# Two heads of an output tile: sums over keys in turns on the halves of the array, retention scores on half rows

## The chip, the cores and the metric

The program runs on one core of a Trainium2 chip. The metric is the device time of one execution in microseconds; several runs of the same program are given by their median.

## The reference, cut to what matters

Two transformer-like blocks run one after the other on 512 tokens of width 1024, in float32. Three attention-like parts are touched by the change:

- **Retention** (first block, 8 heads of 64): the scores q·k are multiplied by a fixed decay of the distance (zero above the diagonal) and then summed over the keys against v, without a softmax; the kernel does this over all 512 tokens at once.
- **NSA** (first block, 8 query heads in 2 key groups): three attentions per head are added with gates: over compressed blocks, over selected blocks and over a window. With 512 tokens the last two are causal softmax attentions with keys and values of their own.
- **MLA** (second block, 8 heads, 96 wide for scores, 64 for values): one causal softmax attention.

```
scores = q @ k.T * decay;  o = scores @ v                  # retention
o = g0 * softmax(q @ kc.T) @ vc + g1 * softmax(q @ ks.T) @ vs + g2 * softmax(q @ kw.T) @ vw   # NSA
o = softmax(q @ k.T / sqrt(96)) @ v                        # MLA
```

## The kernel before, in words

Activations lie transposed: channels on the 128 partitions, 512 tokens along the row. An output tile of an attention is 128 channels x 512 tokens and holds two heads: one on partitions 0 to 63, one on 64 to 127. I call them the low and the high head.

**Softmax attention** (`attn_head`, L406 to L432). For one head and each of four query tiles i of 128 queries: the scores `att_s` over 128(i+1) keys and a mask (L221, the helper behind every `self.mm`), the maximum `att_nm` on VectorE (L419), the exponential `att_e` with its sum on ScalarE (L422), the reciprocal (L424), the scaling (L426 or L428), transposes on TensorE into `att_pt` (L431), and a copy on ScalarE into `PT` (L432), which so holds the probabilities with keys on partitions. `att_pt` has one PSUM bank (`tpc=1`), `att_s` two (`smc=2`), `att_e` three buffers, `PT` two. After the four tiles of a head come its four **sums over keys**, products of 64 value columns with 512, 384, 256 and 128 query columns, into the half of the output tile that is the head's. In NSA (tiles `nsa_o`, p = 0 to 3) the low head comes first with its compressed part (`pct`, `vcz`), then its selected part "s", then its window part "w", and then the high head with the same three; in MLA (`mla_o`) one head after the other. Each output tile is one PSUM bank (`oc=1`).

**Retention** (p = 0 to 3, two heads each). Four projections (`raw`, `project`: three products for each of eight chunks, L216 to L218), rotary embedding, and for each key tile j and each head: scores `ret_s`, a product with the decay `dec` on VectorE into `ret_P` (L686), and the sum `ret_o`. Keys `rk` of both heads lie on 128 rows; the queries are kept twice in `qz`, with zeros on the rows of the other head, so that every score uses all 128 rows of the array. `ret_s` shares two banks with other small products. Behind each p the rows of a modulation vector are summed up (`ada_rows`: 16 loads, ScalarE, GpSimd).

Float32 products are issued as two matmul instructions each; so a head's sums are eight.

**What sets the order.** The order on each engine isn't written by hand. A scheduler walks a simulated time line and, on each engine, takes the instruction of the lowest number among those whose inputs it holds to be there. Numbers follow the program, but an `ahead` block moves them: NSA of p = 0 counts from 4000 before the first retention group, NSA of p = 1 to 3 from the start of retention group p, and MLA, like the preparation of the recurrent part beside it, from a point far ahead in the second block, so that projections of gates fill what they leave. Instructions on one PSUM tile keep the program's order. Transfers are issued on SP's queue in one such order, weights, `dec` and modulation rows alike.

Of the kernel before, what the change touches and what calls it, by code (L numbers as in the profile page):

```python
# [11 lines left out]
F32 = mybir.dt.float32  # L12
# [6 lines left out]
OP = mybir.AluOpType  # L19
# [3 lines left out]
T = 512  # L23
# [135 lines left out]
PRE = ("kc", "vc")  # L159
MS = 2  # L160
PL = ()


class Kernel:
# [238 lines left out]
            nc.tensor.transpose(ps[:, b, :rows], src[:rows, b * 128:(b + 1) * 128], self.cst("ident")[:rows, :rows])  # L403
        nc.scalar.activation(dst, ps[:, :, :rows], AF.Copy)

    def attn_head(self, qk, gate, PT, wk):  # L406

        nc = self.nc  # L410
        for i in range(4):
            n = 128 * (i + 1)
            ps = self.ps([128, T], "att_s")
            w = max(n, 256) if len(qk) > 1 else n
            for j, (q, k) in enumerate(qk):
                self.mm(ps[:, :w], q[:, i * 128:(i + 1) * 128], k[:, :w], j == 0, False)
            self.mm(ps[:, n - 128:n], self.identb, self.maskb, False, True)
            nm = wk.tile([128, 1], F32, name="att_nm", bufs=4)
            nc.vector.tensor_reduce(nm, ps[:, :n], AX.X, OP.max, negate=True)  # L419
            e = wk.tile([128, T], F32, name="att_e", bufs=3)  # L420
            z = wk.tile([128, 1], F32, name="att_z", bufs=4)
            nc.scalar.activation(e[:, :n], ps[:, :n], AF.Exp, bias=nm, accum_out=z)  # L422
            rz = wk.tile([128, 1], F32, name="att_rz", bufs=4)
            nc.vector.reciprocal(rz, z)  # L424
            if gate is None:
                nc.vector.tensor_scalar(e[:, :n], e[:, :n], rz, None, op0=OP.mult)  # L426
            else:
                nc.vector.tensor_scalar(e[:, :n], e[:, :n], rz, gate(i), op0=OP.mult, op1=OP.mult)  # L428
            pt = self.ps([128, 4, 128], "att_pt", "tp")
            for j in range(i + 1):  # L430
                nc.tensor.transpose(pt[:, j, :], e[:, j * 128:(j + 1) * 128], self.cst("ident"))  # L431
            nc.scalar.activation(PT[:, 0:i + 1, i, :], pt[:, 0:i + 1, :], AF.Copy)  # L432

# [25 lines left out]
    def first(self):  # L459
        nc, a = self.nc, self.a  # L460
# [3 lines left out]
        lo_, hi_, full = slice(0, 64), slice(64, 128), slice(0, 128)  # L464
# [10 lines left out]
        tab = {nm: tuple(p.tile([128, T], F32, name=k + nm) for k in ("cos_", "sin_")) for nm, p in (("r", hp), ("n", tp))}  # L475
# [10 lines left out]
        with self.tc.high_priority(offset=5000):  # L486
# [4 lines left out]
            r = self.norm_r(xs, twk, True, True)  # L491
# [10 lines left out]
        wk = self.pool(hid, "wk1")  # L502
# [6 lines left out]
        def raw(name, scale=1.0):  # L509
            o = project(name)  # L510
            q = wk.tile([128, T], F32, name="q_raw", bufs=3)
            nc.scalar.activation(q, o, AF.Copy, scale=scale)
            return q
# [9 lines left out]
        qs = nk.tile([128, 8, T], F32R, name="qs")  # L523
        kk = {nm: nk.tile([128, 2, T], F32R, name="kk" + nm) for nm in "sw"}
        kl = {nm: nk.tile([128, T], F32R, name="kl" + nm) for nm in "sw"}
        vt = {nm: nk.tile([128, 4, 128], F32, name="vt" + nm) for nm in "sw"}
        gt = nk.tile([128, 4, 32], F32, name="gt")
# [10 lines left out]
        for kv, nm in enumerate(("kc", "vc")):  # L538
# [3 lines left out]
            for g in range(2):  # L542
                gr = slice(g * 64, g * 64 + 64)
# [7 lines left out]
            for m in range(16):  # L551
# [3 lines left out]
                for g in range(2):  # L555
                    r = 2 * kv + g
# [7 lines left out]
        w = self.ring("w_raw")  # L564
        nc.sync.dma_start(w, a["w_in"][idx["ngl"]])
        o = self.ps([128, T], "pj", "pj")
        for c in range(NC8):
            r = slice(c % 4 * 32, c % 4 * 32 + 32)
# [87 lines left out]
        rp = self.pool(ns, "ret")  # L656
# [5 lines left out]
        n0 = []  # L662
        for p in range(4):
            n0.append(self.tc.cur_priority)
            qz = rp.tile([128, 2, T], F32, name="qz", bufs=2)
            nc.gpsimd.memset(qz[hi_, 0, :], 0.0)
            nc.gpsimd.memset(qz[lo_, 1, :], 0.0)
            self.rope_T(raw(f"rq{p}"), self.cst("perm_r"), *tab["r"], [(qz[lo_, 0, :], lo_), (qz[hi_, 1, :], hi_)], wk)
            rk = rp.tile([128, T], F32, name="rk", bufs=2)
            self.rope_T(raw(f"rk{p}"), self.cst("perm_r"), *tab["r"], [(rk, full)], wk)  # L670
            rv = rp.tile([128, 4, 128], F32, name="rv", bufs=2)
            self.to_tokens(raw(f"rv{p}"), 128, rv)
            og = project(f"rg{p}")
            th = wk.tile([128, T], F32, name="th", bufs=2)
            nc.scalar.activation(th, og, AF.Tanh, scale=0.5)
            nc.vector.scalar_tensor_tensor(mix[:, p, :], th, 1.0, og, op0=OP.add, op1=OP.mult)
            dec = rp.tile([128, 2, T], F32, name="dec", bufs=2)
            nc.sync.dma_start(dec, a["dec"][:, 2 * p:2 * p + 2, :])
            po = self.ps([128, T], "ret_o", "o")
            for j in range(4):  # L680
                n = T - 128 * j
                for par in range(2):
                    sc = self.ps([128, T], "ret_s")
                    self.mm(sc[:, :n], rk[:, j * 128:(j + 1) * 128], qz[:, par, j * 128:])
                    P = rp.tile([128, T], F32, name="ret_P", bufs=3)
                    nc.vector.tensor_tensor(P[:, :n], sc[:, :n], dec[:, par, :n], op=OP.mult)  # L686
                    self.mm(po[par * 64:par * 64 + 64, j * 128:], rv[:, j, par * 64:par * 64 + 64], P[:, :n], j == 0, j == 3)
            oc = rp.tile([128, T], F32, name="ln_o")
            nc.scalar.activation(oc, po, AF.Copy)
            mu = self.ps([128, T], "ln_mu")  # L690
            self.mm(mu, self.cst("bd64"), oc)
            nc.vector.tensor_tensor(oc, oc, mu, op=OP.subtract)
            sq = rp.tile([128, T], F32, name="ln_sq")
            nc.scalar.activation(sq, oc, AF.Square)
            self.ln_exp()
            var = self.ps([128, T], "ln_var")
            self.mm(var, self.cst("bd64"), sq)
            rs = rp.tile([128, T], F32, name="ln_rs")
            nc.scalar.activation(rs, var, AF.Ln, bias=self.col(5))
            nc.scalar.activation(rs, rs, AF.Exp, scale=-0.5)  # L700
            t = rp.tile([128, T], F32, name="ln_t")
            nc.vector.tensor_scalar(sq, var, 1e-5, None, op0=OP.add)
            self.newton(rs, sq, t)
            nc.vector.scalar_tensor_tensor(t, oc, 0.5, rs, op0=OP.mult, op1=OP.mult)
            nc.vector.tensor_tensor(mix[:, p, :], t, mix[:, p, :], op=OP.mult)

            if p == 0:
                self.ada_rows(a["w_ada"], self.silu1, self.v("b_ada"), mod, 2048, rp, self.ps([128, NC8], "ada_ps", TAG))
                nc.vector.tensor_tensor(self.gg, mod[:, 16:24], self.v("g_post"), op=OP.mult)
            elif p < 3:  # L710
                self.ada_rows(a["w_ada2"], self.silu2, self.v("b_ada2"), self.mod2, (p - 1) * 1024, rp, self.ps([128, NC8], "ada_ps", TAG))
# [3 lines left out]
        for p in range(4):  # L715
            with self.ahead(self.tc.cur_priority - n0[QP[p][0]] - QP[p][1]):
                po = self.ps([128, T], "nsa_o", "o")
                for g in range(2):
                    h = p + 4 * g
                    gr = slice(g * 64, g * 64 + 64)  # L720
                    self.mm(po[gr, :], vcz[:, g, p, :], pct[:, g, :], True, False)
                    for ai, nm in ((1, "s"), (2, "w")):
                        PT = np_.tile([128, 4, 4, 128], F32, name="PT", bufs=2)
                        self.attn_head([(qs[:, h, :], kk[nm][:, g, :]), (qs[gr, h, :], kl[nm][gr, :])], lambda i: gt[:, i, h * 3 + ai:h * 3 + ai + 1], PT, np_)
                        for j in range(4):
                            self.mm(po[gr, j * 128:], vt[nm][:, j, gr], PT[:, j, j:, :], False, ai == 2 and j == 3)
                nc.vector.scalar_tensor_tensor(mix[:, 4 + p, :], po, 0.5, mix[:, 4 + p, :], op0=OP.mult, op1=OP.mult)
        ns.close()
# [83 lines left out]
    def second(self):  # L812
# [279 lines left out]
        with self.ahead(self.tc.cur_priority - n0):  # L1092
            at = self.pool(ax, "mla_at")
            for p in range(4):
                po = self.ps([128, T], "mla_o", "o")
                for par in range(2):
                    h = 2 * p + par
                    PT = at.tile([128, 4, 4, 128], F32, name="PT", bufs=2)
                    self.attn_head([(qf[0:96, h, :], kf[0:96, h, :])], None, PT, at)
                    for j in range(4):  # L1100
                        self.mm(po[par * 64:par * 64 + 64, j * 128:], vt[:, j, h * 64:(h + 1) * 64], PT[:, j, j:, :],
                                j == 0, j == 3)
                nc.scalar.activation(qf[:, 2 * p, :], po, AF.Copy)
# [917 lines left out]
```

## Time and profile before

| | |
|---|---|
| runs | 1384.52, 1402.33, 1398.66 us; median 1398.66 |
| profiled execution | 1399.72 us, its span 1397.9 us (1.8 us lie around it) |
| TensorE (PE) busy | 1285.6 us, 92% of the span |
| VectorE (DVE), ScalarE (ACT), GpSimd (POOL) busy | 859.1 us (61%), 617.6 us (44%), 274.0 us (20%) |
| mean granted TensorE clock | 0.963 of full speed |
| chain of work that ended last | PE 72%, DMA 8%, DVE 7%, ACT 6% |

A busy time counts a matmul from its start to its modelled end, and matmuls overlap in the pipeline: what one costs in a dense stream is the distance from its start to the next start. Retention and NSA lie between 157 and 440 us of the span, MLA between 678 and 803 us.

### The profile page before, as it was taken

To read this page: it belongs to the slowest core of one execution; us is meant where nothing else is said; L and a number is where in the kernel's file an instruction comes from. 1 tells how busy PE (TensorE), PEld (TensorE's weight loads), DVE (VectorE), ACT (ScalarE), POOL (GpSimd) and SP (SyncE) were. 2 spreads that over 40 slices of the span, in tenths; PEclk is the share of its full clock that TensorE was granted. 3 is DMA by queue.
4 is the path that set the end of the run, shared out by engine and by line. 5 is a ranking of instruction groups with operands and counts; after the bars stand their busy time and mean duration, and the time that the engine had idled before them with its cause. 6 is when DMAs were issued, how large, how long until landed. Compare 5 with 4: busy or idle time off the path is not lost.

```text
span 1397.9 us, 20781 instructions
## 1 busy us (share of the span) xinstructions
PE 1285.6 (92%) x7765; PEld 1009.1 (72%) x7765; DVE 859.1 (61%) x1971; ACT 617.6 (44%) x1204; POOL 274.0 (20%) x237
## 2 busy tenths in 40 slices
PE   4899999999998999999999899988998779998887
PEld 1468656566556986887677578887997777888777
DVE  6646553754764555444867764647574965997832
ACT  5234453655453557334465644545333543342010
POOL 0000140423000100000000034434000214436560
PEclk9999999999999999999999979999999999999799
DMA  9532341333111113223332154545233536878564
GB/s 346 192 99 76 122 150 60 121 121 106 61 68 61 46 63 107 83 83 106 113 106 91 61 155 148 174 129 159 84 100 106 173 106 194 329 256 307 168 216 120
DMA packets 92110, 187.56 MB, mean 134 GB/s; under 512 B 11084, under 2 KB 37260, under 8 KB 92000
## 3 DMA queue, kind: packets, MB, share of 16 engines
q1 hardware_dynamic: 77744, 143.84, 32.2%
q0 software_dynamic: 14256, 42.30, 8.9%
q8 instruction: 63, 1.03, 0.3%
q14 instruction: 47, 0.39, 0.1%
HBM read 178.94 MB, written 16.78 MB: 140 GB/s over the span
## 4 chain that ended last, share of the span: by engine, by line
PE 72%; DMA 8%; DVE 7%; ACT 6%; issue 3%; POOL 2%; SPq 0%; ACTq 0%; DVEq 0%; POOLq 0%
PE pj L216 11%; PE pj L217 11%; PE pj L218 11%; PE y L221 6%; DMA ada_w<-in_w_ada 5%; PE att_s L221 4%; PE nsa_o L221 3%; PE lv L221 3%; PE att_pt L431 2%; POOL ada_acc L300 2%; PE ret_s L221 2%; PE ret_o L221 2%; PE mr L221 1%; PE mla_o L221 1%; ACT ada_w L298 1%
## 5 line engine op out<-in xcount | busy, mean ns | idle before, releaser
L216 PE MATMUL pj<-hh,w_hi 128*128 128x512 f32 (+1 forms) x736 | 284.1, 388 | 15.6 <-ACT hh L357 8.2
L217 PE MATMUL pj<-hl,w_hi 128*128 128x512 f32 (+1 forms) x736 | 282.5, 384 | 2.9 <-DVE hl L358 2.9
L218 PE MATMUL pj<-hh,w_lo 128*128 128x512 f32 (+1 forms) x736 | 282.2, 384 | 0.4 <-DVE w_lo L211 0.4
L300 POOL TENSOR_TENSOR ada_acc<-ada_acc,ada_w 128x512 f32<-128x512 f32 x98 | 130.5, 1337 | 380.1 <-ACT ada_w L298 361.6
L211 DVE TENSOR_TENSOR w_lo<-w_raw,w_hi 128x1024 fp32r<-128x1024 f32 (+1 forms) x108 | 133.0, 1234 | 102.2 <-ACT w_hi L210 93.4
L216 PEld LDWEIGHTS pj<-hh,w_hi 128*128 128x128 f32 x736 | 141.1, 192 | 48.9 <-issue 11.3
L210 ACT ACTIVATE w_hi<-w_raw 128x1024 fp32r<-128x1024 f32 (+1 forms) x112 | 114.4, 1025 | 128.7 <-PE pj L217 103.3
L217 PEld LDWEIGHTS pj<-hl,w_hi 128*128 128x128 f32 x736 | 141.1, 192 | 32.9 <-DVE hl L358 6.6
L218 PEld LDWEIGHTS pj<-hh,w_lo 128*128 128x128 f32 x736 | 140.8, 191 | 28.6 <-issue 3.0
L298 ACT ACTIVATE ada_w<-ada_w,silu 128x512 f32<-128x512 f32 x98 | 70.4, 722 | 97.1 <-DMA ada_w<-in_w_ada 94.5
L221 PE MATMUL y<-dg,up 128*128 128x128 f32 x768 | 101.1, 295 | 12.6 <-DMA up<-in_eu,gix 5.6
L221 PEld LDWEIGHTS y<-dg,up 128*128 128x128 f32 x768 | 97.7, 210 | 14.7 <-DMA up<-in_eu,gix 5.8
L419 DVE TENSOR_REDUCE att_nm<-att_s 128x1 f32<-128x128 f32 (+1 forms) x96 | 46.6, 486 | 73.3 <-PE att_s L221 72.9
L432 ACT ACTIVATE PT<-att_pt 128x128 f32<-128x128 f32 (+1 forms) x96 | 41.7, 434 | 89.8 <-PE att_pt L431 89.7
L1411 DVE SCALAR_TENSOR_TENSOR junk<-dn,htok 128x1024 f32<-128x1024 f32 x48 | 58.5, 1219 | 15.4 <-DMA dn<-in_ed_rows,gix 10.7
L422 ACT ACTIVATE att_e<-att_s,att_nm 128x128 f32<-128x128 f32 (+1 forms) x96 | 50.5, 526 | 11.2 <-DVE att_nm L419 10.5
L431 PE MATMUL att_pt<-consts,att_e 128*128 128x128 f32 x240 | 44.6, 285 | 4.4 <-ACT PT L432 2.7
L1405 POOL DMA_INDIRECT dn<-in_ed_rows,gix x32 | 34.9, 1092 | 59.3 <-DVE gix L1444 36.6
L431 PEld LDWEIGHTS att_pt<-consts,att_e 128*128 128x128 f32 x240 | 29.1, 141 | 23.0 <-issue 8.5
L216 PE MATMUL pj<-oh,w_hi 128*128 128x256 f32 x128 | 39.8, 311 | 2.9 <-DVE m_g L1157 2.9
L1405 POOL DMA_INDIRECT up<-in_eu,gix x32 | 35.5, 1109 | 14.3 <-issue 8.2
L217 PE MATMUL pj<-ol,w_hi 128*128 128x256 f32 x128 | 37.7, 295 | 0.0
(617 smaller groups left out, 2701.6 us busy)
## 6 DMA issues: line engine op xcount, KB each, us to landing
ada_w<-in_w_ada SPq DMA_DIRECT2D x144, 256.0 KB, 3.3
w_raw<-in_w_in SPq DMA_DIRECT2D x65, 512.0 KB, 3.8
w_raw<-in_w_out SPq DMA_DIRECT2D x24, 512.0 KB, 4.0
w_raw<-in_w_query SPq DMA_DIRECT2D x16, 512.0 KB, 5.5
w1t<-in_cmp_w SPq DMA_DIRECT2D x8, 512.0 KB, 4.2
gate_d<-g_t SPq DMA_DIRECT2D x16, 256.0 KB, 2.0
w_raw<-in_w_o_rwkv SPq DMA_DIRECT2D x8, 512.0 KB
x<-in_xT SPq DMA_DIRECT2D x4, 512.0 KB, 8.6
```

Of the source, the lines that this page charges most:

```text
L210: self.nc.scalar.activation(hi, src, AF.Copy)
L211: (eng or self.nc.vector).tensor_tensor(lo, src, hi, op=OP.subtract)
L216: self.nc.tensor.matmul(ps, wh, xh, start=(i == 0), stop=False)
L217: self.nc.tensor.matmul(ps, wh, xl, start=False, stop=False)
L218: self.nc.tensor.matmul(ps, wl, xh, start=False, stop=(i == n - 1))
L221: self.nc.tensor.matmul(ps, l, r, start=start, stop=stop)
L298: nc.scalar.activation(wt if k else t, wt, AF.Copy, scale=s[:, k:k + 1])
L300: nc.gpsimd.tensor_tensor(t, t, wt, op=OP.add)
L422: nc.scalar.activation(e[:, :n], ps[:, :n], AF.Exp, bias=nm, accum_out=z)
L431: nc.tensor.transpose(pt[:, j, :], e[:, j * 128:(j + 1) * 128], self.cst("ident"))
L1405: nc.gpsimd.indirect_dma_start(out=g, out_offset=None, in_=a[table], in_offset=bass.IndirectOffsetOnAxis(ap=ix, axis=0), **more)
L1411: nc.vector.scalar_tensor_tensor(junk, g, 1.0, h, op0=OP.mult, op1=OP.mult, accum_out=out)
```

## The change

For each output tile, both heads are now taken through the softmax before any of their sums over keys, and the sums then alternate: low head j = 0, high head j = 0, low head j = 1, and so on. In NSA this is done for the selected part of both heads and then for the window part, and the compressed parts of both heads come first. `PT` has three buffers. In MLA `att_e` has two buffers in place of three, and the small columns three in place of four. In retention the queries `rq` are kept once, the scores of a head are a product over its own 64 rows, the scores of both heads are issued before both products with the decay, and the sums alternate. The zero fills of `qz` are gone, one of two additions of the rotary embedding of q as well, and `dec` has one buffer in place of two.

```diff
+NPT = 3
...
-    def attn_head(self, qk, gate, PT, wk):
+    def attn_head(self, qk, gate, PT, wk, eb=3, sb=4):
...
-            e = wk.tile([128, T], F32, name="att_e", bufs=3)
-            z = wk.tile([128, 1], F32, name="att_z", bufs=4)
+            e = wk.tile([128, T], F32, name="att_e", bufs=eb)
+            z = wk.tile([128, 1], F32, name="att_z", bufs=sb)
...
-            qz = rp.tile([128, 2, T], F32, name="qz", bufs=2)
-            nc.gpsimd.memset(qz[hi_, 0, :], 0.0)
-            nc.gpsimd.memset(qz[lo_, 1, :], 0.0)
-            self.rope_T(raw(f"rq{p}"), self.cst("perm_r"), *tab["r"], [(qz[lo_, 0, :], lo_), (qz[hi_, 1, :], hi_)], wk)
+            rq = rp.tile([128, T], F32, name="rq", bufs=2)
+            self.rope_T(raw(f"rq{p}"), self.cst("perm_r"), *tab["r"], [(rq, full)], wk)
...
-            dec = rp.tile([128, 2, T], F32, name="dec", bufs=2)
+            dec = rp.tile([128, 2, T], F32, name="dec")
...
+                scs, Ps = [], []
+                for gr in (lo_, hi_):
+                    sc = self.ps([128, T], "ret_s")
+                    self.mm(sc[:, :n], rk[gr, j * 128:(j + 1) * 128], rq[gr, j * 128:])
+                    scs.append(sc)
                 for par in range(2):
-                    sc = self.ps([128, T], "ret_s")
-                    self.mm(sc[:, :n], rk[:, j * 128:(j + 1) * 128], qz[:, par, j * 128:])
                     P = rp.tile([128, T], F32, name="ret_P", bufs=3)
-                    nc.vector.tensor_tensor(P[:, :n], sc[:, :n], dec[:, par, :n], op=OP.mult)
-                    self.mm(po[par * 64:par * 64 + 64, j * 128:], rv[:, j, par * 64:par * 64 + 64], P[:, :n], j == 0, j == 3)
+                    nc.vector.tensor_tensor(P[:, :n], scs[par][:, :n], dec[:, par, :n], op=OP.mult)
+                    Ps.append(P)
+                for gr, P in zip((lo_, hi_), Ps):
+                    self.mm(po[gr, j * 128:], rv[:, j, gr], P[:, :n], j == 0, j == 3)
...
-                for g in range(2):
-                    h = p + 4 * g
-                    gr = slice(g * 64, g * 64 + 64)
+                for g, gr in enumerate((lo_, hi_)):
                     self.mm(po[gr, :], vcz[:, g, p, :], pct[:, g, :], True, False)
-                    for ai, nm in ((1, "s"), (2, "w")):
-                        PT = np_.tile([128, 4, 4, 128], F32, name="PT", bufs=2)
-                        self.attn_head([(qs[:, h, :], kk[nm][:, g, :]), (qs[gr, h, :], kl[nm][gr, :])], lambda i: gt[:, i, h * 3 + ai:h * 3 + ai + 1], PT, np_)
-                        for j in range(4):
+                for ai, nm in ((1, "s"), (2, "w")):
+                    PTs = []
+                    for g, gr in enumerate((lo_, hi_)):
+                        h = p + 4 * g
+                        PTs.append(np_.tile([128, 4, 4, 128], F32, name="PT", bufs=NPT))
+                        self.attn_head([(qs[:, h, :], kk[nm][:, g, :]), (qs[gr, h, :], kl[nm][gr, :])], lambda i: gt[:, i, h * 3 + ai:h * 3 + ai + 1], PTs[g], np_)
+                    for j in range(4):
+                        for gr, PT in zip((lo_, hi_), PTs):
                             self.mm(po[gr, j * 128:], vt[nm][:, j, gr], PT[:, j, j:, :], False, ai == 2 and j == 3)
...
-                for par in range(2):
-                    h = 2 * p + par
-                    PT = at.tile([128, 4, 4, 128], F32, name="PT", bufs=2)
-                    self.attn_head([(qf[0:96, h, :], kf[0:96, h, :])], None, PT, at)
-                    for j in range(4):
+                PTs = []
+                for h in (2 * p, 2 * p + 1):
+                    PTs.append(at.tile([128, 4, 4, 128], F32, name="PT", bufs=NPT))
+                    self.attn_head([(qf[0:96, h, :], kf[0:96, h, :])], None, PTs[-1], at, 2, 3)
+                for j in range(4):
+                    for par, PT in enumerate(PTs):
+                        h = 2 * p + par
                         self.mm(po[par * 64:par * 64 + 64, j * 128:], vt[:, j, h * 64:(h + 1) * 64], PT[:, j, j:, :],
                                 j == 0, j == 3)
```

## Rows read from the trace of the kernel before

**Rows 1.** Busy time by stretch: stretch and length, then each engine, clock, DMA.
```profile
157.00:440.00 283.00, 274.74 (x1138) 166.11 (x1139) 160.15 (x333) 145.57 (x313) 59.54 (x46) 0.98 0.29 93
678.00:803.00 125.00, 119.47 (x531) 81.73 (x530) 88.18 (x241) 75.33 (x185) 0.00 (x0) 1.00 0.28 93
```

**Rows 2.** Groups by line on PE: busy us, mean ns, idle before.
```profile
L221 PE MATMUL ret_s<-qz,rk 128*128 128x512 f32 (+3 forms) x64 | 24.3, 472 | 0.0
L221 PE MATMUL ret_o<-ret_P,rv 128*64 128x512 f32 (+3 forms) x64 | 23.7, 458 | 0.0
...
L221 PE MATMUL nsa_o<-PT,vts 128*64 128x512 f32 (+3 forms) x64 | 20.6, 468 | 1.1 <-ACT PT L432 1.1
...
L221 PE MATMUL mla_o<-PT,vt 128*64 128x512 f32 (+3 forms) x64 | 18.9, 439 | 1.2 <-ACT PT L432 1.2
```

**Rows 3.** Timeline of PE, 736 to 740 us: start, length, what.
```profile
736.36 0.40 PE L217 MATMUL pj<-hl,w_hi 128*128 128x512 f32 x1
736.59 0.40 PE L218 MATMUL pj<-hh,w_lo 128*128 128x512 f32 x1
736.91 2.37 PE L221 MATMUL mla_o<-PT,vt 128*64 128x512 f32 x8
739.21 0.33 PE L431 MATMUL att_pt<-consts,att_e 128*128 128x128 f32 x1
```

**Rows 4.** Timeline of PE, 418 to 421 us.
```profile
418.39 1.93 PE L221 MATMUL nsa_o<-PT,vtw 128*64 128x512 f32 x5
419.95 0.64 PE L221 MATMUL nsa_o<-pct,vcz 128*64 128x512 f32 x1
420.16 0.49 PE L221 MATMUL nsa_o<-PT,vtw 128*64 128x256 f32 x2
...
420.96 0.33 PE L431 MATMUL att_pt<-consts,att_e 128*128 128x128 f32 x1
```

**Rows 5.** Timeline of PE, 880 to 882 us: products over 64 rows, later stage.
```profile
880.02 0.60 PE L221 MATMUL mr<-AR,KA 64*128 64x256 f32 x4
880.45 0.59 PE L221 MATMUL mr<-AR,BE 64*128 64x256 f32 x2
880.88 0.59 PE L221 MATMUL mr<-AR,KA 64*128 64x256 f32 x2
881.41 0.33 PE L1206 MATMUL r_tp<-consts,AR 128*128 128x128 f32 x1
```

**Rows 6.** Timeline of PE, 258 to 280 us, retention and NSA of p = 1.
```profile
258.45 1.88 PE L221 MATMUL ret_s<-qz,rk 128*128 128x512 f32 x4
...
260.86 1.07 PE L221 MATMUL nsa_o<-pct,vcz 128*64 128x512 f32 x2
...
262.23 1.07 PE L221 MATMUL ret_o<-ret_P,rv 128*64 128x512 f32 x2
...
268.22 1.07 PE L221 MATMUL ret_o<-ret_P,rv 128*64 128x512 f32 x2
...
277.20 2.37 PE L221 MATMUL nsa_o<-PT,vts 128*64 128x512 f32 x8
```

**Rows 7.** Timeline of DVE, 260 to 264 us.
```profile
260.78 0.68 DVE L686 TENSOR_TENSOR ret_P<-ret_s,dec 128x512 f32<-128x512 f32 x1
...
263.11 0.68 DVE L686 TENSOR_TENSOR ret_P<-ret_s,dec 128x512 f32<-128x512 f32 x1
```

**Rows 8.** Timeline of ACT: the fourth copies into PT of two successive heads.
```profile
271.79 0.60 ACT L432 ACTIVATE PT<-att_pt 128x512 f32<-128x512 f32 x1 [2.66 <-PE att_pt L431]
...
296.44 0.57 ACT L432 ACTIVATE PT<-att_pt 128x512 f32<-128x512 f32 x1
```

**Rows 9.** Timeline of ACT, 766 to 772 us, two exponentials of one MLA head.
```profile
766.67 0.57 ACT L422 ACTIVATE att_e<-att_s,att_nm 128x384 f32<-128x384 f32 x1
...
771.46 0.69 ACT L422 ACTIVATE att_e<-att_s,att_nm 128x512 f32<-128x512 f32 x1
```

**Rows 10.** Timeline of SP's queue, 226 to 227 us.
```profile
226.19 0.38 SPq L678 DMA_DIRECT2D dec<-in_dec  x1
```

More of the change, by code (lines that the diff above doesn't have):

```diff
@@ L417, in attn_head @@
             self.mm(ps[:, n - 128:n], self.identb, self.maskb, False, True)
-            nm = wk.tile([128, 1], F32, name="att_nm", bufs=4)
+            nm = wk.tile([128, 1], F32, name="att_nm", bufs=sb)
             nc.vector.tensor_reduce(nm, ps[:, :n], AX.X, OP.max, negate=True)
-            e = wk.tile([128, T], F32, name="att_e", bufs=3)
-            z = wk.tile([128, 1], F32, name="att_z", bufs=4)
+            e = wk.tile([128, T], F32, name="att_e", bufs=eb)
+            z = wk.tile([128, 1], F32, name="att_z", bufs=sb)
             nc.scalar.activation(e[:, :n], ps[:, :n], AF.Exp, bias=nm, accum_out=z)
-            rz = wk.tile([128, 1], F32, name="att_rz", bufs=4)
+            rz = wk.tile([128, 1], F32, name="att_rz", bufs=sb)
             nc.vector.reciprocal(rz, z)
```

## The prediction

> **What bounds the kernel now.** I read the busy times by stretch first. In the two stretches that the change touches, TensorE is busy 274.7 of 283 us and 119.5 of 125 us, VectorE and ScalarE at most 71% [rows 1]. So TensorE's stream is the limit, and a product saved there is time saved as long as something else is ready to take its place; in both stretches projections do. The groups by line name what the change works on: `ret_s`, `ret_o`, the two groups of `nsa_o` sums and `mla_o`, 64 matmuls each, some 19 to 24 us busy each [rows 2]. The timeline then gives the price of one, since busy times count overlaps twice.
>
> **Sums over keys today.** A head's eight matmuls run from 736.91 to the next start at 739.21, which is 2.30 us; entering costs 0.32 us after a projection product where products follow each other at 0.23, so 0.09 us more [rows 3]. I put the change of shape at 0.1 us on the way in and 0.1 us on the way out, which leaves 2.2 us of array time: 1280 columns, 512 of them (0.4, or 0.88 us) in j = 0. One visit costs 2.39 us, two heads 4.78 us. There are 24 head parts: 16 in NSA, 8 in MLA, so 12 pairs.
>
> **Do halves of the columns run side by side?** Yes, in one place of this trace. Behind the low head's last sums stands the high head's compressed product, two matmuls on the other half of the same bank. It starts at 419.95, while three sums are still to come, and the whole group ends at 420.96: 2.57 us from 418.39, where the eight alone take 2.30 and the two alone 1.00 (260.86 to the next product at 261.86, an interval that its row's 1.07 us length covers) [rows 3, 4, 6]. So 0.73 of the 1.00 us are hidden. The Trainium skill (TensorE: Matmul & The Clock Gate, Part 3, The mechanism) says that a weight load overlaps running matmuls only where the row groups differ. Two column halves have the same rows, so by that rule each half would wait for the other's matmul before its own load, and the sums would save nothing. [rows 4] disagree with it, and the row decides.
>
> **How much of a pair will meet?** This is where I chose. The sums of a pair stand together in the program, but the order on TensorE is laid by readiness. Instructions on one bank keep the program's order, yet none waits for its successors: the first compressed product of p = 1 goes out at 260.86, and the sums that follow it in its bank start at 277.20 [rows 6]. It is so for all four p. In the new order the low head's j = 0 sum needs only the low `PT`. That is complete 25 us before the next head's at p = 1 (fourth copies at 271.79 and 296.44) [rows 8], and where less fills TensorE the distance shrinks to one head's chain, not to nothing. Its number is lower than that of the retention work beside it, which runs ahead of the attention: the decay products of p = 1 begin at 260.78, before that first head is through [rows 7, 8]. So I expect it to go out alone; the low head's j = 1 then has to wait in its bank for the high head's j = 0. A pair costs 0.88 + 0.2 for the lone sum, then the high head's full 2.2 us with the low head's other three hidden beside it, plus 0.2: 3.48 us. Saved: 4.78 - 3.48 = 1.3 us. NSA 8 x 1.3 = 10.4 us, MLA 4 x 1.3 = 5.2 us. The bounds are 2.39 us a pair if all sums meet (28.7 us for twelve) and 0 if none does.
>
> **Compressed products.** Today a p pays 1.00 us for the first and 0.27 for the second. Both are ready when the bank is free, so they meet: 0.27 x 4 = 1 us saved.
>
> **Retention scores.** On half rows a score takes as long as before unless its partner runs beside it. Side by side is possible: four products over 64 rows take 0.43 us (880.02 to 880.45), and the same 0.43 us passes for only two at 880.45 [rows 5]. Leaving that shape costs 0.1 us (0.53 in place of 0.43 at 880.88), entering I take to be the same. The first two scores of a p stand together already, four matmuls at 258.45 [rows 6], some 0.43 us each, 1.72 us; halved and with 0.2 for the shape they save 0.66, four times: 2.6 us. The later ones wait for banks that the decay products free one at a time. These are 2.3 us apart even for j = 0, where both scores are there (260.78 and 263.11) [rows 7], since other VectorE work stands between, and the sums that follow are 6 us apart (262.23 and 268.22) [rows 6]. So I expect 24 later scores to go alone, each paying 0.1 to 0.2 us for its shape: 2.4 to 4.8, taken as 3.6 us. Scores together: -1 us. Retention's sums: 0. The bounds: if every pair meets, sums save half of 8 x 2.2 us and 16 visits of 0.2, 12 us, and scores 8.8 - 16 x 0.2 = 5.6 us; if no scores meet, 32 x 0.2 = 6.4 us are lost.
>
> **Buffers and the rest.** In MLA two `att_e` buffers stand where three are used up today: a head's fourth exponential starts at 771.46, 4.2 us after the third has ended (766.67 + 0.57) [rows 9], when the first transposes free a buffer. With two, the third waits as well. ScalarE and VectorE do other work meanwhile, so I charge 0.25 us for each of eight heads, 2 us, between 0 and 6. The one `dec` buffer: today the load for p = 2 goes out at 226.19, when the last decay product of p = 0 has freed its buffer [rows 10]; with one buffer it is the load for p = 1 that goes then. Its first product is at 260.78 [rows 7]: 34 us cover it, and weight loads queued behind it on SP would wait only as long as that last product is late. The fewer VectorE and GpSimd instructions (four additions, put at 0.68 us like the products of [rows 7], and eight fills) lie beside TensorE's work: nothing. Were VectorE the limit, they would give 2.7 us.
>
> **Sum.** 10.4 + 5.2 + 1 - 1 - 2 = 13.6 us of TensorE's time, which is 97 and 96% busy there [rows 1]: 13 us. 1399.72 - 13 = 1386.7; the profiled run lies 1.1 us above the median, so 1386 against 1398.66, 0.9% faster. What comes next in line is TensorE again. The forecast's own range is 1378 to 1394 (scores and ring at their bounds, a few us of reshuffled order either way).
>
> **Rivals.**
> - *All pairs meet.* The scheduler finds the high head ready, or fills TensorE with other work until then, and the decay products stand together. Then 28.7 + 1 + 12 + 5.6 - 2 = 45 us, about 43 on the path: 1357. For it: the loads of both halves do overlap [rows 4]. Against it: [rows 6, 8]. Chance 0.20.
> - *The change does not do what it says.* If products on different halves of a bank aren't kept in order, the low head's four sums all go early, as today. Left are 1 - 1 - 2 us: about 1401. Against it: the second compressed product never passes the sums ahead of it, though its inputs are there long before. Chance 0.14.
> - *Weight loads of column halves do not overlap in alternation*, the rule named above, as a mechanism of this kernel: the sixteen matmuls of a pair run one after the other, 4.4 us as today, also 1401. Against it: [rows 4]. Chance 0.04.
> - *The `att_e` ring takes over in MLA, and the kernel is slower.* Place: L422 in 760 to 803 us, 16 query tiles. If each third tile's wait is exposed, a tile pays up to the chain from one exponential to its transposes, some 1.4 us (0.69 for the exponential [rows 9] and, estimated from it, as much again for sum, reciprocal and scaling): 22 us. 1399.72 + 22 - 15.6 = 1406. It decides from 1 us a tile (16 us) on. For it: the ring is full today [rows 9]. Against it: the other engines' work fills the wait. Chance 0.10.
>
> **How the numbers follow.** Forecast 0.50, rivals 0.20, 0.14, 0.04, 0.10; 0.02 for other outcomes. The range of 8 in 10 runs from 1357, which takes in most of the first rival, to 1404, which takes in the second and third. About 2% (28 us) is what a measurement of this kernel can tell from no change: faster than 1370.7 are the first rival and a sliver of the forecast, 0.22; slower than 1426.6 only a tail of the last, 0.03; the rest 0.75.
>
> **What would show it.** Right: in the profile after, `nsa_o` and `mla_o` sums stand as two matmuls alone and, microseconds later, fourteen together that last about 2.3 us. Sixteen together in 2.3 us would be the first rival, eight and eight the second, sixteen in 4.4 us the third. `ret_s` would be 64*128, four together only for j = 0, otherwise two. In 678 to 803 us a growing wait of L422 or of the transposes for it would be the last. I am wrong if the scheduler's simulated readiness differs from what I read out of the trace: then the number of sums that meet is another, and with it the largest term.

## The result, and the profile after

The kernel after took 1377.81 us (median of 4 runs, 1370.59 to 1383.79) against 1398.13: ratio 0.9858, 95% interval 0.982 to 0.9896. Timed again beside the kernel before on one chip (the last experiment), it took 1378.46 against 1394.21: 0.988, 0.9849 to 0.9911. The forecast was 1386, 13 us less; measured are 20 us less, and 16 the second time. The first median lies 0.2 us below the forecast's own range of 1378 to 1394, the second inside it. By the 2% bound this is no change, the case that had the most chance. Two of the ten runs of the experiment e2 (1406.49 and 1408.29 us) fell in a slower state, over 1.5% above its fastest, and are left out of every figure below.

The busy times of the same two stretches of work, in the profile after (span 1374.7 us), answer to [rows 1]:

```profile
157.00:425.00 268.00, 261.14 (x1144) 159.65 (x1144) 158.73 (x330) 144.97 (x313) 57.42 (x42) 0.99 0.31 98
660.00:785.00 125.00, 114.02 (x527) 79.23 (x525) 87.51 (x240) 79.65 (x188) 0.00 (x0) 1.00 0.27 88
```

NSA's last sum starts at 421.5 us where it was 437.8, and TensorE still is 97% busy up to there. In MLA's 125 us it is busy for 114.0 us where it was for 119.5: there its idle time has doubled. The groups by line on PE (busy us, mean ns, idle before) answer to [rows 2]; the columns of the first two are as there:

```profile
L222 PE MATMUL ret_o<-ret_P,rv 128*64 128x512 f32 (+3 forms) x64 | 23.2, 458 | 0.0
L222 PE MATMUL ret_s<-rq,rk 64*128 64x512 f32 (+3 forms) x64 | 20.5, 482 | 0.0
L222 PE MATMUL mla_o<-PT,vt 128*64 128x256 f32 (+3 forms) x64 | 13.8, 442 | 1.4 <-ACT PT L433 1.4
L222 PE MATMUL nsa_o<-PT,vtw 128*64 128x256 f32 (+3 forms) x64 | 13.8, 442 | 0.7 <-ACT PT L433 0.7
L222 PE MATMUL nsa_o<-PT,vts 128*64 128x256 f32 (+3 forms) x64 | 13.8, 442 | 0.3 <-ACT PT L433 0.3
```

The mean of a single sum has hardly moved (442 ns against 439 to 468), while the group's busy time fell from 18.9 or 20.6 to 13.8 us: the same matmuls lie on top of each other. Retention's sums are as they were. PE's timeline shows how:

```profile
187.25 1.07 PE L222 MATMUL nsa_o<-PT,vts 128*64 128x512 f32 x2
188.26 0.38 PE L222 MATMUL att_s<-kkw,qs 128*128 128x256 f32 x1
...
199.99 1.13 PE L222 MATMUL ret_s<-rq,rk 64*128 64x512 f32 x4
201.05 0.66 PE L432 MATMUL att_pt<-consts,att_e 128*128 128x128 f32 x4
...
202.46 1.07 PE L222 MATMUL ret_o<-ret_P,rv 128*64 128x512 f32 x2
203.46 0.91 PE L222 MATMUL ret_s<-rq,rk 64*128 64x384 f32 x2
204.30 2.37 PE L222 MATMUL nsa_o<-PT,vts 128*64 128x512 f32 x14
206.60 0.33 PE L432 MATMUL att_pt<-consts,att_e 128*128 128x128 f32 x1
...
263.21 1.08 PE L222 MATMUL nsa_o<-pct,vcz 128*64 128x512 f32 x4
264.22 0.38 PE L222 MATMUL att_s<-kks,qs 128*128 128x256 f32 x1
...
693.64 1.07 PE L222 MATMUL mla_o<-PT,vt 128*64 128x512 f32 x2
694.65 0.70 PE L222 MATMUL att_s<-kf,qf 96*128 96x512 f32 x1
...
715.27 2.37 PE L222 MATMUL mla_o<-PT,vt 128*64 128x512 f32 x14
717.57 0.33 PE L432 MATMUL att_pt<-consts,att_e 128*128 128x128 f32 x1
```

The low head's j = 0 sum goes out alone (two matmuls, 1.01 us), and the other fourteen follow later, together in 2.30 us, the time that eight took before [rows 3]. All twelve pairs stand like this, 17 to 23 us apart for five of them and 5 to 12 for the rest. The four compressed products take 1.01 us, which two took alone [rows 6].

### The profile page after: what moved, and what is told of

It reads as the page before. It is cut to its first block, busy times and chain, and to the rows that moved or that the text cites. A ratio compares the mean times of both kernels' runs of the same rounds, so it can differ in the third digit from the quotient of the medians.

```text
span 1374.7 us, 20778 instructions
## 1 busy us (share of the span) xinstructions
PE 1259.4 (92%) x7765; PEld 994.5 (72%) x7765; DVE 851.1 (62%) x1967; ACT 619.1 (45%) x1206; POOL 269.5 (20%) x229
## 4 chain that ended last, share of the span: by engine, by line
PE 62%; DMA 11%; DVE 7%; issue 7%; ACT 6%; POOL 5%; SPq 0%; DVEq 0%; ACTq 0%; POOLq 0%
PE pj L217 9%; PE pj L218 9%; PE pj L219 9%; DMA ada_w<-in_w_ada 6%; PE y L222 4%; PE att_s L222 4%; PE lv L222 3%; POOL ada_acc L301 2%; POOL dn L1413 2%; PE nsa_o L222 2%; PE att_pt L432 2%; PE ret_o L222 1%; ACT ada_w L299 1%; PE ada_ps L222 1%; PE z L222 1%
## 5 line engine op out<-in xcount | busy, mean ns | idle before, releaser
L219 PE MATMUL pj<-hh,w_lo 128*128 128x512 f32 (+1 forms) x736 | 278.9, 379 | 0.4 <-DVE w_lo L212 0.4
L222 PEld LDWEIGHTS y<-dg,up 128*128 128x128 f32 x768 | 97.8, 208 | 13.6 <-issue 7.2
L1419 DVE SCALAR_TENSOR_TENSOR junk<-dn,htok 128x1024 f32<-128x1024 f32 x48 | 58.6, 1221 | 19.3 <-DMA dn<-in_ed_rows,gix 14.1
```

The costliest lines, as they stand in the source:

```text
L219: self.nc.tensor.matmul(ps, wl, xh, start=False, stop=(i == n - 1))
L222: self.nc.tensor.matmul(ps, l, r, start=start, stop=stop)
L1419: nc.vector.scalar_tensor_tensor(junk, g, 1.0, h, op0=OP.mult, op1=OP.mult, accum_out=out)
```

## How the runs are compared

The runs of one kernel differ by up to 18 us, and most of that follows TensorE's granted clock, which every run records as a mean: with two levels, 2 x (1 - mean) x span is the time at 1.2 GHz. Over 110 runs of all the kernels here, with the mean of each kernel in each set of runs on one chip taken out, a microsecond at 1.2 GHz goes with 0.36 us of time (standard error 0.02). The last column takes this out: it is the difference from the kernel before in the same set at equal clock, with a standard error of some 1 to 1.6 us. It is an estimate: 0.36 is a mean over all the places where the clock falls, and it is used here also between kernels whose clock falls in different places.

| run | what it is | median us (runs) | ratio, 95% interval | us at 1.2 GHz, mean | against before at equal clock |
|---|---|---|---|---|---|
| e13_after | the kernel after | 1378.46 (6) | 0.988, 0.9849 to 0.9911 | 93 | -15.8 |
| e5_no_turns | after without the turns | 1410.25 (4) | 1.0082, 1.0063 to 1.0101 | 113 | +5.4 |
| e2_ret_alone | retention's part alone | 1391.76 (8) | 0.9971, 0.9936 to 1.0007 | 92 | -2.6 |
| e10_nsa_ret | retention's and NSA's part | 1397.94 (10) | 0.9958, 0.9927 to 0.9989 | 118 | -14.1 |
| e9_before_ring | before with the small rings | 1408.89 (4) | 1.0109, 1.0058 to 1.0159 | 113 | +7.8 |
| e6_mla_high | high head first in MLA | 1370.54 (4) | 0.982, 0.9758 to 0.9882 | 88 | -22.8 |
| e1_high_first | the same in NSA and MLA | 1383.84 (4) | 0.9874, 0.9844 to 0.9904 | 113 | -18.6 |
| e4_all_high_first | the same in retention too | 1386.26 (4) | 0.991, 0.9885 to 0.9934 | 138 | -26.2 |
| e7_high_fill | e4 and 32 products more | 1368.59 (4) | 0.983, 0.9772 to 0.9887 | 103 | -27.9 |
| e12_best | e7 again | 1372.51 (6) | 0.9837, 0.9809 to 0.9866 | 105 | -24.5 |
| e8_after_fill | after and 32 products more | 1377.74 (4) | 0.9865, 0.9819 to 0.9911 | 90 | -15.9 |
| e11_mla_two | e6 with two `PT` in MLA | 1381.07 (4) | 0.9835, 0.9784 to 0.9886 | 109 | -26.3 |

The kernel before had 94 to 97 us at 1.2 GHz in each set.

## Experiments: is it the turns?

Theory A is the forecast's: the sums of two heads on the two column halves pass at the same time, and the array time saved is time of the kernel. Its rival B is that the saving comes from what else the change rearranges.

**e5_no_turns** keeps all of the change but the turns (the same in MLA):

```
-                    for j in range(4):
-                        for gr, PT in zip((lo_, hi_), PTs):
+                    for gr, PT in zip((lo_, hi_), PTs):
+                        for j in range(4):
                             self.mm(po[gr, j * 128:], ...)
```

> The changed kernel, but in NSA and MLA the low head's four sums stand before the high head's four. Theory A: nothing meets, 12 x 1.3 = 15.6 us are lost again, about 1392 us. Theory B: the second head's chain still starts before the sums of the first, so about 1378 us.

It took 1410.25 us, more than the kernel before. The order of two loops is worth 21 us at equal clock. B is out. In the stages that the edit touches, the profiles of e5 and of the kernel after, one execution each, differ by less: from the first to the last product on `nsa_o` they have 278.9 and 264.5 us, from MLA's first score to its last sum 130.1 and 125.2. That is 19.3 us, with 10.3 us less at 1.2 GHz, so 15 to 16 us at equal clock, where 15.6 were forecast. The rest lies in stages that the edit leaves alone, and why is open. That e5 is slower than before, where A expected 1392, needed another cause, which e9 found.

**e2_ret_alone** puts the new retention block into the kernel before.

> The kernel before with retention's part of the change alone (queries once, scores on half rows and both first, sums in turns, one decay buffer). Theory A by its sum: four first pairs of scores save 2.6 us, 24 others lose 2.4 to 4.8: 1 us slower than before, about 1399 us. Rival: entering and leaving the half-row shape costs more than read, 0.4 us a visit as in the attention scores: 28 x 0.4 - 2.6 = 8 us slower, 1406 us. Rival the other way: a good part of the gain of the whole change is here, 1388 us.

1391.76 us, 2.6 less than before at equal clock, where 1 us more was forecast; the interval of the ratio takes in 1. Retention's part is worth little, but its sign was not the forecast's.

**e10_nsa_ret** takes MLA back to the old order and rings.

```
-                PTs = []
-                for h in (2 * p, 2 * p + 1):
-                    PTs.append(at.tile(..., name="PT", bufs=NPT))
-                    self.attn_head(..., PTs[-1], at, 2, 3)
-                for j in range(4):
-                    for par, PT in enumerate(PTs):
+                for par in range(2):
+                    h = 2 * p + par
+                    PT = at.tile(..., name="PT", bufs=2)
+                    self.attn_head(..., PT, at)
+                    for j in range(4):
```

> The kernel after with MLA attention as before (a head's sums right behind the head, two buffers for the transposed exponentials, three for the exponentials), so NSA's and retention's part of the change alone. Reading S (the stages of the profiles: MLA's part of the change nets about 3 us of gain, its ring included): about 1381 (1377 to 1385), slower than the kernel after. Reading M (the medians of the ring's own run: the ring costs some 13 us and the turns give 5 to 7 back, so that MLA's part nets a loss of 6 to 8): about 1371 (1366 to 1374), faster than the kernel after.

Both readings missed: 1397.94 us. At equal clock NSA's part is worth 14.1 - 2.6 = 11.5 us, and MLA's 15.8 - 14.1 = 1.7 net, which is no more than its error of 1.6. As measured its ratio is 0.8% (11 us) worse than that of e13, the kernel after; some 9 of these go with the clock, 118 us at 1.2 GHz against 93. The windows over the stage that follows MLA, which the edit doesn't touch (though the order of some projections in it shifts), show where. First the kernel after, then e10:

```profile
784.00:997.00 213.00, 196.50 (x1842) 176.05 (x1841) 124.14 (x243) 98.71 (x198) 72.98 (x56) 0.96 0.47 143
```

```profile
784.00:1014.00 230.00, 208.04 (x1862) 186.86 (x1861) 133.69 (x250) 102.11 (x202) 74.19 (x56) 0.92 0.45 135
```

Clock 0.92 for 230 us is 37 us at 1.2 GHz; 0.96 for 213 is 17. The 20 us more at half the clock can make up for at most 10 of the 17 us by which the stage is longer. Why the clock falls more there with MLA's old order, and what the remaining 7 us are, stays open.

**e9_before_ring** measures the disputed cost by itself, in the kernel before:

```
-            e = wk.tile([128, T], F32, name="att_e", bufs=3)
+            e = wk.tile([128, T], F32, name="att_e", bufs=2 if gate is None else 3)
```

and three in place of four for the small columns.

> The kernel before with MLA's exponentials on two buffers in place of three and its small columns on three in place of four, the sums as before: the ring's cost by itself. The forecast charged 2 us for it, with ends 0 and 6: 1401, between 1399 and 1405. If it is slower than 1406, the ring takes back most of what the turns give MLA.

1408.89 us: 13.6 more, of which 7.8 remain at equal clock, with an error of 1.6; the forecast's upper end was 6. The waits for the exponentials in MLA (who waited for `att_e`, us and times) show the mechanism, first before, then with the small rings:

```profile
  DVE att_rz L424: 6.7, 7
  PE att_pt L431: 1.7, 1
```

```profile
  DVE att_rz L424: 14.1, 12
  PE att_pt L431: 5.6, 6
```

VectorE's reciprocal waits twice as long for the exponentials, and TensorE's transposes behind it wait 5.6 us where they waited 1.7. This fits e5: retention's -2.6 and the ring's +7.8 make +5.2 against +5.4 measured.

By whole runs, MLA's turns would be worth 1.7 + 7.8 = 9.5 us. The stage itself shows less. From MLA's first score to the end of its last sum, TensorE has the same 530 matmuls in every version; in order the kernel before, e9, e5, the kernel after and e6 (an experiment of the next section):

```profile
678.10:802.80 124.70, 119.17 (x530) 81.60 (x530) 88.08 (x241) 75.04 (x184) 0.00 (x0) 1.00 0.28 93
678.40:810.40 132.00, 122.24 (x530) 82.82 (x530) 87.37 (x241) 78.36 (x186) 0.00 (x0) 0.97 0.28 90
673.50:803.60 130.10, 121.54 (x530) 82.08 (x530) 88.13 (x241) 78.19 (x186) 0.00 (x0) 0.99 0.28 93
658.10:783.30 125.20, 114.22 (x530) 79.77 (x529) 88.86 (x241) 78.57 (x186) 0.00 (x0) 1.00 0.27 91
659.20:781.50 122.30, 112.19 (x530) 79.03 (x530) 87.86 (x241) 78.43 (x186) 0.00 (x0) 0.99 0.30 97
```

The small rings alone lengthen the stage by 7.3 us (124.7 to 132.0, 6.8 us of it at 1.2 GHz), and by 5.4 in e5 (3.4 at 1.2 GHz): 4 to 5 us at equal clock, within the forecast's bounds. The turns take 4.9 us off again (e5 to the kernel after), some 4 at equal clock. From the kernel before to the one after, TensorE's busy time falls by 5.0 us, but its idle time grows from 5.5 to 11.0: the stage is 0.5 us longer. These lengths repeat: 124.7 us in e2 and e10, which have MLA's old order and rings, and 125.2 in e13 and e8. So the ring takes back all that the turns give MLA, and the rest of what whole runs put on either lies outside the stage.

## Experiments: the lone sum, and where its time goes

The forecast's first rival had all sixteen sums meet. That can be had: the high head is the later one, so if its sum stands first in each turn, no low sum can leave ahead of it.

```
-                        for gr, PT in zip((lo_, hi_), PTs):
+                        for gr, PT in zip((hi_, lo_), PTs[::-1]):
```

**e1_high_first** does it in NSA and MLA (there as `for par in (1, 0)`), **e4_all_high_first** in retention too, **e6_mla_high** in MLA alone.

> The changed kernel, with one thing altered: in NSA and MLA the high head's sum stands first in each turn, so that no sum can go out before both heads are through. Theory A (what is saved is TensorE's time in which halves of the array run side by side, and the lone sum of each of 12 pairs costs 0.88 + 0.2 us of it): 12 x 1.08 = 13 us less than the changed kernel, about 1365 us, and sixteen sums together in about 2.3 us. Theory B (the gain came from the second head's chain no longer standing behind the first head's sums, not from halves side by side): that is as in the changed kernel, so about 1377 us.

> As the kernel with the high head first in NSA and MLA, and the same order in retention's sums, so that these stand in pairs too. Theory A: 16 pairs meet, up to 8.8 us of array time and some 12 visits of 0.2 us less, about 10 us below the former, 1355 us. Theory B: no gain from meeting, and retention's low sums wait longer: 1377 us or a little more.

> The kernel after with the high head's sum first in MLA attention alone, so that all eight sums of a tile's pair go in pairs there; NSA and retention as in the kernel after. Theory A (a lone sum's 0.9 to 1.3 us is time of the stage): four tiles, 4 to 5 us less, 1373. Theory C (the stage has gaps, and the lone sum lies in one or keeps the clock): no gain, 1376 to 1380; if the granted clock falls in the MLA stage too, up to 1384.

The sums do meet; in the timeline of e6 sixteen take the 2.31 us of eight:

```profile
716.76 2.37 PE L222 MATMUL mla_o<-PT,vt 128*64 128x512 f32 x16
719.07 0.70 PE L222 MATMUL z<-gd,w_gu 128*128 128x256 f32 x2
```

In MLA the lone sum's time is time of the stage: it takes 122.3 us in e6 and, with the same order, 122.0 to 122.9 in e1, e4, e7 and e12, against 125.2 in the kernel after, e13 and e8. That is 2.9 us, or some 4 at equal clock (3.4 us of e6's stage are at 1.2 GHz), where four lone sums of 1.0 to 1.3 us promised 4 to 5. The whole run, 1370.54 us, is 7.0 less than the kernel after at equal clock, with an error of some 2; as measured the intervals of the ratios overlap. In NSA it is not time of the kernel: e1 (0.9874 of before) and e4 (0.991) are no faster than the kernel after (0.9858 and 0.988), though e4's groups of sums on PE are much shorter than those of the kernel after:

```profile
L222 PE MATMUL ret_o<-ret_P,rv 128*64 128x512 f32 (+3 forms) x64 | 13.6, 506 | 1.7 <-DVE ret_P L688 1.6
L222 PE MATMUL nsa_o<-PT,vts 128*64 128x512 f32 (+3 forms) x64 | 11.7, 516 | 0.9 <-ACT PT L433 0.9
L222 PE MATMUL nsa_o<-PT,vtw 128*64 128x512 f32 (+3 forms) x64 | 11.3, 501 | 1.4 <-ACT PT L433 1.4
L222 PE MATMUL mla_o<-PT,vt 128*64 128x512 f32 (+3 forms) x64 | 9.5, 439 | 0.9 <-ACT PT L433 0.9
```

The means of NSA's rows have risen to 501 and 516 ns: part of these sums ran at 1.2 GHz. The windows over NSA's last tiles (PE first, then PEld, DVE, ACT, POOL, the granted clock, DMA) show it, the kernel after first:

```profile
350.00:360.00 10.00, 10.00 (x49) 6.81 (x47) 6.81 (x15) 3.87 (x10) 0.00 (x0) 1.00 0.18 55
360.00:370.00 10.00, 9.45 (x31) 3.54 (x30) 8.89 (x16) 9.41 (x17) 0.00 (x0) 1.00 0.16 52
370.00:380.00 10.00, 9.68 (x45) 4.73 (x45) 6.38 (x18) 3.05 (x9) 0.00 (x0) 1.00 0.34 105
```

Then e4:

```profile
350.00:360.00 10.00, 8.85 (x36) 3.79 (x35) 8.29 (x16) 8.90 (x18) 0.00 (x0) 1.00 0.17 52
360.00:370.00 10.00, 10.00 (x28) 4.36 (x26) 5.84 (x16) 2.37 (x8) 0.00 (x0) 0.51 0.33 105
370.00:380.00 10.00, 10.00 (x40) 5.25 (x40) 4.63 (x12) 5.16 (x12) 0.00 (x0) 0.64 0.00 0
```

The last projection ends at 360 us in the kernel after and at 351 in e4; in the 10 us behind it, ScalarE and VectorE are busy for 8.3 to 9.4 us and TensorE has short gaps. In e4 TensorE was busy 8.85 of 10 us in the stretch before the clock fell, in the kernel after 9.45 in the one where it held. Of the 47 us more at 1.2 GHz in e4's profile than in that of the kernel after, 38 lie between NSA's first and last product. Theory C: with the sums packed, TensorE has less to do here, the clock falls to 1.2 GHz, and the products that follow take back what was saved. Its rival R: the high-first order itself waits longer, and the clock only follows.

**e7_high_fill** gives TensorE of e4 useless work in NSA's last two tiles: the first product of each score tile is done once more ahead of the real one, which overwrites it.

```
+            for _ in range(again):
+                self.mm(ps, qk[0][0][:, i * 128:(i + 1) * 128], qk[0][1][:, :T], True, True)
             for j, (q, k) in enumerate(qk):
```

> The kernel after with the high head's sum first everywhere (as in the earlier run, 1386 us), and in the last two output tiles of NSA attention each score tile's first product runs twice at its full 512 columns, the second time over the first: 32 products more of about 0.25 us, 8 us of TensorE work that nothing needs. Theory C (the saved lone sum came back as a lower granted clock in the emptier tail): the granted clock from 340 to 430 us stays at or near 1.00 where it was at half for 37 us, and the time falls in spite of the added work, to about 1372 (1364 to 1379). Rival R (the high-first order itself waits longer, and the clock is only a sign of that): the clock stays low or the added work is paid, 1386 to 1394.

**e8_after_fill** does the same to the kernel after.

> The kernel after with the same 32 doubled products and nothing else: a control, whose clock in that stretch was already at 1.00. Theory C: the added work can only cost, from nothing (all in gaps) to 8 us: 1378 to 1386, taken 1381. Rival R says the same here. If it is faster than the kernel after by more than 4 us, the filling helps in some way other than by the clock of that stretch.

With 32 products more, e7 took 1368.59 us where e4 took 1386.26. They ran on different chips: against the kernel before beside each, the ratios are 0.983 and 0.991, some 11 us apart. Their intervals overlap by a hair (0.9772 to 0.9887, 0.9885 to 0.9934); that of e12, the program of e7 again, lies clear of e4's (0.9809 to 0.9866). The same stretch in e7:

```profile
350.00:360.00 10.00, 10.00 (x49) 4.70 (x45) 5.78 (x11) 6.37 (x11) 0.00 (x0) 1.00 0.13 41
360.00:370.00 10.00, 9.24 (x43) 4.78 (x41) 9.47 (x24) 5.67 (x15) 0.00 (x0) 1.00 0.40 118
370.00:380.00 10.00, 9.90 (x53) 5.23 (x53) 4.62 (x13) 6.59 (x17) 0.00 (x0) 1.00 0.00 0
```

e8, whose clock was at 1.00 anyway, gained nothing (1377.74). So the filling helps through the clock: 138 us at 1.2 GHz in e4, 103 in e7, and at equal clock the two are the same within their error (-26.2, -27.9). If the clock only followed, e7 would have had to pay for its products. C holds in the mean and not in each execution: the profile of e12, the same program, has 0.66 from 360 to 380 us. That of e11, in which TensorE's order over NSA is that of the kernel after, has 0.76 there, after the same busy 10.00 and 9.45 us in the two stretches before. So what TensorE did in this stretch doesn't decide alone. Nor does C put R out: at equal clock e1 is 4 us behind e6, so the high head first in NSA seems to cost time of its own, and e4 is 8 ahead of e1, which retention's pairs would give. Together they are 3 us ahead of e6, where 8 lone sums at 1.08 us and some 10 us for retention promised 18. The error of such a difference is some 2 us, and what the order costs in NSA stays open.

**e11_mla_two** tries to have MLA's pairs without the small rings: two `PT` buffers and three of `att_e`, four of the small columns.

> The kernel with the high head first in MLA (1370.5 us), but with two buffers for the transposed exponentials in place of three, and three for the exponentials in place of two, as they were before the change. If the ring of two costs what its own run showed (4 us in the stage, up to 13 by the medians) and two buffers hold nothing up: 1357 to 1367, taken 1362. Rival: with two buffers the next tile's first copy waits for the sums of both heads, some 2 us for each of four tiles, as much as the ring gives: 1368 to 1376.

At equal clock it gains 3.5 us on e6, and in MLA's stage 1.7 (120.6 us against 122.3); as measured it is 1381.07, behind e6, with 109 us at 1.2 GHz against 88. No verdict on the buffers.

**e12_best and e13_after** set e7 beside the kernel after on one chip.

> The version with the high head first everywhere and the doubled products in NSA's last two tiles (1368.6 us before), again, beside the kernel after on the same chip, to settle whether it beats it. Theory C: it is ahead of the kernel after by 6 to 12 us. Taking out of every run the time at half clock (a us of it has cost 0.39 us over the runs so far), by 11 to 14. Rival: no difference beyond the interval.

> The kernel after, unchanged. With retention's part (e2) worth 1.6 us, NSA's (e10 against e2) 13 and MLA's 1.5 net, all at equal clock, it should come out 16 us under the kernel before at equal clock, and 13 to 23 under it as measured. If it is more than 23 or less than 13 at equal clock, the parts don't add up.

1372.51 against 1378.46: 6 us ahead in the medians, 8.7 at equal clock, but as measured the intervals of the two ratios overlap. e13's -15.8 is what the parts add up to by construction, since MLA's was taken from it (the parts as named in its expectation were taken with all ten runs of e2); the independent tests of the sum are e5 and the stage lengths above.

## Why the prediction was right

- **TensorE is the limit, and a product saved is time saved.** Right for the turns: the loop order alone is worth 15 to 16 us in the two stages and 21 in the whole run (e5). Its premise, "as long as something else is ready", has limits: with the small rings TensorE stands idle in MLA for 5.5 us more than before, and in NSA's last tiles e1 and e4 took more off the sums and ended no earlier.
- **Halves of the columns run side by side.** Right. Fourteen and sixteen matmuls in 2.3 us; the rival from the weight loads would have shown 4.4. The Trainium skill (TensorE: Matmul & The Clock Gate, Part 3, The mechanism) has, in its list of what overlaps, a load overlap running matmuls only across different row groups; here both halves use all rows, and the traces, with sixteen matmuls in 2.31 us, don't agree with it.
- **How much of a pair will meet.** Right to the matmul: two alone, fourteen together, all twelve times. A pair now takes 1.01 + 2.30 = 3.31 us where two visits of 2.30 stood: 1.29 saved, forecast 1.3.
- **NSA.** 10.4 for the sums and 1 for the compressed products, 11.4 us; measured 11.5 at equal clock.
- **MLA.** Net 5.2 - 2 = 3.2 us of gain forecast; the stage became 0.5 us longer. The turns were sized rightly: TensorE's busy time fell by 5.0 us. The ring's charge was the weakest step. It rested on "ScalarE and VectorE do other work meanwhile", but in the trace TensorE's transposes wait for the exponentials, and the ring cost 4 to 5 us of the stage where 2 were charged. So the fourth rival names what happened inside MLA, at a price of 4 to 5 us and not of 22.
- **Retention.** 1 us of loss forecast, 2.6 us of gain measured at equal clock. The first four scores take 1.06 us (199.99 to 201.05), which is 0.86 and 0.2 for the shape, as worked out; the later ones go by twos. The sums stayed alone. Where the 3.6 us between forecast and measurement come from isn't shown; the shorter list of VectorE and GpSimd work, put at nothing, is one candidate.
- **The sum.** 13.6 us forecast, 15.8 at equal clock, 16 in the second measurement. That it comes so near is partly luck: MLA gave 1.5 to 4 us less than forecast, and retention 3.6 more. The first measurement's 20 has one run of four at a mean clock of 0.979 in it (1370.59 us), and the profiles compared first, 1399.72 and 1376.66 us, had mean clocks of 0.963 and 0.967, 103 and 91 us at 1.2 GHz.
- **The first rival**, all meet, 1357: e4 brings the sums together and is worth 26 us at equal clock, not 43; its scores stay mostly in twos (`ret_s`, 20.5 us busy after, is no shorter in e4), and the clock takes half of the 26 back. The rival priced the packing, and neither what packing does to the clock nor what the order costs in NSA.

## What to carry to other kernels

Look in the timeline for two products on different halves of a bank: if they already overlap once, a loop order that lets them take turns is worth its array time where TensorE has other work to go on with. Whether the head that is ready last should stand first in each turn has to be tried: it helped in MLA and not in NSA. Give a ring that is full its own measurement before you shrink it to make room; here it cost more than twice its estimate, all that MLA gained. Read such a cost over its own stage: whole runs, which differ by more than it, made it 8 us, the stage 4 to 5. And read the granted clock over the stretch where an engine was relieved: work taken from TensorE where nothing fills its place can come back as a lower clock.

## What the runs showed of the hardware that was not expected

- Matmuls over 128 rows on the two column halves, alternating, overlap completely: sixteen take 2.31 us, eight take 2.30.
- Less work for TensorE was more time: e4 to e7 adds 32 products and goes from 0.991 to 0.983 of the kernel before, some 11 us, with 35 us less at 1.2 GHz.
- A microsecond at 1.2 GHz went with 0.36 us over 110 runs of these kernels, and the same program differs by up to 46 us in it from run to run (e1: mean clocks of 0.952 to 0.968). Kernels that differ by 1% should be compared at equal clock as well.
